# Units of the SSD stage traced behind single weight pieces, convolutions and output step among them

## The chip, the cores and the metric

The kernel runs on one core of a Trainium2 chip. The time is device microseconds of one execution, and the lower the better. The program is one launch with no communication between cores. Matmuls run on TensorE (PE in the profile), elementwise work on VectorE (DVE) and ScalarE (ACT), loads are issued by SyncE (SP).

## The reference, cut to what matters

Two decoder layers over 256 tokens of width 2048. Layer 0 is a Mamba-2 mixer (the SSD stage), layer 1 a dilated attention. The change lies in layer 0:

```python
proj = h @ in_w                                   # 2048 -> z (4096), x (4096), B and C (8 groups x 128 each), dt (64)
xBC = silu(causal_depthwise_conv(xBC, conv_w, conv_b))   # 4 taps
dt = softplus(dt + dt_bias);  A = -exp(A_log)
# one chunk of 256 tokens: for each of 8 groups g (8 heads of 64 columns each)
cb    = C[g] @ B[g].T                             # scores
decay = exp(acum[l] - acum[s]) for l >= s         # per head
y     = (cb * decay) @ (x * dt)  +  x * D         # output step
y     = y * silu(z)
y     = y * rsqrt(mean(y*y over the group) + eps) * norm_g
out   = y @ out_w                                 # 4096 -> 2048
```

## The kernel before, in words

Every product is made in three passes of half precision halves: a weight piece of 128 x 1024 numbers (512 KB) is loaded to `raw`, ACT copies it to `whi` (L100), DVE makes the remainder `wlo = raw - whi` (L102), and PE multiplies the high and low halves with those of the activations. `raw` has six buffers, `whi` and `wlo` have four each. So the copy of piece p+4 can start only when PE is through with piece p, and PE is never more than four pieces behind ACT and DVE.

The program is recorded through helpers, and a scheduler then sets the order of instructions on each engine at build time; each engine works strictly through its own list. `tc.issue_after(i)` pins instructions behind i on i's engine.

The mixer's input product is done in groups. A group's weights come in up to three products: `bc` (B and C of two groups), `xs` (x of one group) and `z` (its gate). `cm_quad` takes pieces of two k-tiles with 24 matmuls each (L151 to L153); `cm_wide`, which is used for x from group 2 on, takes pieces of four k-tiles with 8 matmuls of 512 columns and 8 of 256 (L194, L197), eight pieces for a group. Products that a first stage has begun (`begun`) have fewer pieces left.

For each group there are then these steps, and it is these that the change moves:

- the convolution `conv` of one 128-row tile: ACT scales (L389), DVE adds three taps (L392), ACT takes SiLU (L394). There are four tiles of x for a group and four of B and C for two groups;
- `scores`: two matmuls, then DVE L742 and L743;
- `stage1`: ACT makes the decays `seg` in two halves of eight RELU each (L757) and an EXP (L759), and `grow` (L761); DVE multiplies with the scores (L762). `seg` has two buffers. It ends with eight transposes of x on PE (L770), `xd` and `xo` on DVE (L772, L777) and four scalings on ACT (L781);
- `stage2`, the group's output step: 4 matmuls for `po` and 16 for `py` on PE (L791, L802), then on DVE L793, L794, L805 twice and L806 (the gate), and a square on ACT (L808);
- `stage3`: sums of squares on DVE (L813, L815), two small matmuls with ones (L818), and a reciprocal root of twelve small DVE instructions (L820, L278 to L284), sent to HBM by a POOL queue.

In the loop over g the code of one turn is written in this order: the product `bc` (on odd g), `scores`, the product `xs` of group g+1, stage3 of g-1, stage1 of g, the four convolutions of x of g+1, the product `z` of g+1, stage2 of g. Each stands between whole products. `background` puts the dot products of the adaLN gate (L320, 1 MB of weights each) between pieces. At the end the product `z` of group 7 runs with the last scores inside it, and then stage2 of group 7. The output product (`out_pieces`, L228) follows: its first pieces need `y` of group 0, 1 and so on, scaled by L871 and split by ACT L878 and DVE L879 (`ylo`). stage3 of group 7 is called there at the second piece, with high priority.

Of the kernel before, what the change touches and what calls it, by code (L numbers as in the profile page):

```python
# [9 lines left out]
F32 = mybir.dt.float32  # L10
# [13 lines left out]
G = 8  # L24
# [25 lines left out]
def trunk(ctx, tc, xT, x, c, par, cst, bias, lnrow, ada, wdt, win, wxs, wout, wk, wv, wbin, wbout, out):  # L50
# [55 lines left out]
    upcoming, ready, owed = [], [], []  # L106
# [72 lines left out]

    def cm_wide(src, dst, rate=(0, 1), moving=None, later=False, seen=lambda a: a):  # L180
# [3 lines left out]
        for q in range(KT // 4):  # L184
# [6 lines left out]
            for k in range(4):  # L191
# [4 lines left out]
                for n in range(2):  # L196
                    T.matmul(ps[n][:, 0, :], lo[:, k, n * P:n * P + P], high(kt), start=False, stop=kt == KT - 1,  # L197
                             skip_group_check=True)
            background(*rate)
        def put():  # L200
# [158 lines left out]
    with ExitStack() as cA:  # L359
# [13 lines left out]
        with ExitStack() as cS:  # L373
# [11 lines left out]
            def conv(ps, ct, dst):  # L385
# [4 lines left out]
                for j in (2, 1, 0):  # L390
                    o = 3 - j
                    V.scalar_tensor_tensor(acc[:, o:], ps[:, :L - o], w[:, j:j + 1], acc[:, o:],  # L392
                                           op0=ALU.mult, op1=ALU.add)
                S.activation(dst, acc, AF.Silu)  # L394

            def bc_conv(g, t):
                for i in range(2):
                    bc[g + i] = p0.tile([P, 2, L], F32, name="bcm", bufs=3)
                    conv(t[2 * i], 32 + g + i, bc[g + i][:, 0, :])
                    conv(t[2 * i + 1], 40 + g + i, bc[g + i][:, 1, :])  # L400

            def xs_conv(g, t):
                xs[g] = xst[g]
                for i in range(4):
                    conv(t[i], 4 * g + i, xs[g][:, i, :])
# [4 lines left out]
            def xs_wide(g):  # L410
# [6 lines left out]
                def convolve():  # L417
                    for n in range(4):
                        conv(t[:, n, :], 4 * g + n, t[:, n, :])

                return convolve

            def product(kind, g, pre=None):
# [25 lines left out]
                if kind == "xs":  # L449
                    return lambda: xs_conv(g, t)  # L450
                bc_conv(g, t)

            with ExitStack() as c0:
# [243 lines left out]
                bc_conv(0, tiles(first[0]))  # L697
                xs_conv(0, tiles(first[1]))
# [47 lines left out]
            def stage1(g, cb):  # L746

                segs, grow = [], px.tile([P, 4, P], F32, name="grow", bufs=1)
                for w in range(2):
# [15 lines left out]
                    segs.append(seg)  # L765
                xd = px.tile([P, 2, 512], F32, name="xd", bufs=1)
                for b in range(2):
                    px_ = aux.tile([P, 512], F32, name="aux")
                    for i in range(4):
                        T.transpose(px_[:, i * P:i * P + P], xs[g][:, i, b * P:b * P + P], ident)  # L770
                    heads = px_.rearrange("p (h e) -> p h e", h=HPG)
                    V.tensor_tensor(xd[:, b, :].rearrange("p (h e) -> p h e", h=HPG), heads,  # L772
                                    dtT[:, b, g * HPG:(g + 1) * HPG, None].to_broadcast([P, HPG, 64]),
                                    op=ALU.mult)
                    if b == 0:
# [714 lines left out]
```

## Time and profile before

| what | value |
|---|---|
| median of three runs | 1239.31 us (1236.56 to 1241.85) |
| the profiled execution | 1240.34 us, span 1238.5 us |
| PE busy | 1210.6 us (98% of the span) |
| DVE busy | 1026.3 us (83%) |
| ACT busy | 711.5 us (57%) |
| mean granted clock of PE | 0.994 |
| 200 to 545 us (where the change lies): PE, DVE, ACT busy | 329.5, 304.7, 269.8 of 345.0 us |

The rows of the profile give the start and length of instructions in microseconds of the span; in brackets stands the engine's idle time just ahead of them and what ended it. A window's row gives the busy time of each engine in that stretch, the count of its instructions behind x, then the clock that PE was granted (1.00 is full speed) and the DMA share. A matmul's time in a row runs on into the next one's, so pieces are measured from first matmul to first matmul.

### The profile page before, as it was taken

The page shows a single profiled execution, that of the slowest core. Times are in us where ns is not written, and L with a number is a line of the kernel's source. Part 1 is how long each engine was busy: PE and PEld are TensorE (multiplying, and loading weights), DVE is VectorE, ACT ScalarE, POOL GpSimd, SP SyncE. Part 2 cuts the span into 40 slices and gives each one's busy share as a digit, 9 for nine tenths or more (in the row PEclk, how much of TensorE's full clock was granted, in tenths as well). Part 3 has the DMA queues.
Part 4 walks back from the last instruction along what each step waited for, and adds up shares of the span by engine and source line. Part 5 has one row for each costly group of instructions (what it writes and reads, how often), then busy time and mean ns, then how long its engine had stood idle before and what let it go on. Part 6 is the DMA issues. An engine that isn't in the chain of part 4 may idle for free.

```text
span 1238.5 us, 20144 instructions
## 1 busy us (share of the span) xinstructions
PE 1210.6 (98%) x7772; PEld 1074.9 (87%) x7772; DVE 1026.3 (83%) x1450; ACT 711.5 (57%) x1056; POOL 12.5 (1%) x21
## 2 busy tenths in 40 slices
PE   8999999899999999979999999999999999999998
PEld 8999999888999998868888888888888888888886
DVE  6999987899888999999788678788996885756886
ACT  4555467787698899644344365443444844444751
POOL 0000000000000000000000000000000000000001
PEclk9999999999999999989999999999999999999999
DMA  9999976785767658689898668989997785355563
GB/s 374 421 421 422 422 273 232 250 312 162 217 227 200 153 204 209 145 255 358 324 370 337 244 221 320 352 347 361 373 392 283 276 269 175 115 188 170 189 257 68
DMA packets 81969, 337.06 MB, mean 272 GB/s; under 512 B 9537, under 2 KB 10321, under 8 KB 69073
## 3 DMA queue, kind: packets, MB, share of 16 engines
q1 hardware_dynamic: 80496, 333.59, 75.3%
q0 software_dynamic: 1168, 2.11, 1.0%
q8 instruction: 61, 1.00, 0.3%
q14 instruction: 36, 0.29, 0.1%
q10 hardware_dynamic: 208, 0.08, 0.0%
HBM read 332.50 MB, written 3.24 MB: 271 GB/s over the span
## 4 chain that ended last, share of the span: by engine, by line
PE 73%; DVE 11%; ACT 7%; DMA 6%; issue 3%; SPq 0%; DVEq 0%; ACTq 0%
PE acc L228 23%; PE acc L194 21%; PE acc L197 11%; DMA raw<-in_win 3%; DVE wlo L102 3%; DVE araw L320 3%; PE acc L153 3%; PE acc L151 3%; PE acc L152 3%; ACT whi L100 2%; DVE cacc L392 2%; DMA araw<-in_ada 2%; ACT seg L757 1%; PE py L802 1%; PE acc L238 1%
## 5 line engine op out<-in xcount | busy, mean ns | idle before, releaser
L100 ACT ACTIVATE whi<-raw 128x1024 fp32r<-128x1024 f32 x389 | 408.1, 1057 | 345.0 <-PE acc L194 105.7
L102 DVE TENSOR_TENSOR wlo<-raw,whi 128x1024 fp32r<-128x1024 f32 x389 | 470.2, 1221 | 135.9 <-ACT whi L100 130.5
L194 PE MATMUL acc<-actT,whi 128*128 128x512 f32 x1280 | 401.4, 394 | 0.0
L197 PEld LDWEIGHTS acc<-actT,wlo 128*128 128x128 f32 x1280 | 239.5, 188 | 54.5 <-DVE wlo L102 2.3
L197 PE MATMUL acc<-actT,wlo 128*128 128x256 f32 x1280 | 254.8, 280 | 1.5 <-DVE wlo L102 1.3
L153 PE MATMUL acc<-actT,wlo 128*128 128x256 f32 x884 | 242.1, 279 | 7.9 <-DVE wlo L102 7.9
L151 PE MATMUL acc<-actT,whi 128*128 128x256 f32 x884 | 245.4, 280 | 1.3 <-ACT whi L100 0.7
L152 PE MATMUL acc<-actT,whi 128*128 128x256 f32 x884 | 244.6, 278 | 0.0
L320 DVE SCALAR_TENSOR_TENSOR araw<-araw,cb__72 128x2048 f32<-128x2048 f32 x95 | 217.1, 2285 | 2.0 <-DMA araw<-in_ada 1.7
L194 PEld LDWEIGHTS acc<-actT,whi 128*128 128x128 f32 x1280 | 194.8, 188 | 0.6
L153 PEld LDWEIGHTS acc<-actT,wlo 128*128 128x128 f32 x884 | 164.8, 189 | 10.1 <-DVE wlo L102 9.9
L151 PEld LDWEIGHTS acc<-actT,whi 128*128 128x128 f32 x884 | 166.9, 189 | 2.9 <-ACT whi L100 0.9
L152 PEld LDWEIGHTS acc<-actT,whi 128*128 128x128 f32 x884 | 166.9, 189 | 0.2 <-issue 0.2
L228 PE MATMUL acc<-whi,actT 128*128 128x512 f32 x560 | 144.4, 392 | 0.5 <-ACT whi L100 0.5
L228 PEld LDWEIGHTS acc<-whi,actT 128*128 128x128 f32 x560 | 105.1, 189 | 23.0 <-ACT whi L100 0.9
L228 PE MATMUL acc<-wlo,actT 128*128 128x512 f32 x384 | 104.1, 393 | 0.0
L228 PEld LDWEIGHTS acc<-wlo,actT 128*128 128x128 f32 x384 | 72.7, 189 | 16.0
L228 PE MATMUL acc<-whi,ylo 128*128 128x512 f32 x208 | 57.4, 399 | 1.4 <-DVE ylo L879 1.4
L228 PEld LDWEIGHTS acc<-whi,ylo 128*128 128x128 f32 x208 | 39.7, 191 | 10.1 <-DVE ylo L879 1.5
L757 ACT ACTIVATE seg<-cbc,cumT 128x128 f32<-128x128 f32 x128 | 40.9, 388 | 5.1 <-PE py L802 3.4
L392 DVE SCALAR_TENSOR_TENSOR cacc<-xs,prm,cacc 128x255 f32<-128x255 f32 (+2 forms) x84 | 37.4, 478 | 2.4 <-ACT cacc L389 2.1
L524 ACT ACTIVATE htmp<-xt,mod 128x256 f32<-128x256 f32 x16 | 9.6, 600 | 31.0 <-DVE mod L325 29.3
(331 smaller groups left out, 1092.6 us busy)
## 6 DMA issues: line engine op xcount, KB each, us to landing
araw<-in_ada SPq DMA_DIRECT2D x96, 1024.0 KB, 7.5
raw<-in_win SPq DMA_DIRECT2D x109, 512.0 KB, 9.4
raw<-in_wout SPq DMA_DIRECT2D x64, 512.0 KB, 7.2
raw<-in_wbin SPq DMA_DIRECT2D x64, 512.0 KB, 4.0
raw<-in_wxs SPq DMA_DIRECT2D x48, 512.0 KB, 4.7
raw<-in_wv SPq DMA_DIRECT2D x48, 512.0 KB, 7.2
raw<-in_wk SPq DMA_DIRECT2D x48, 512.0 KB, 7.7
cbc<-cumd SPq DMA_DIRECT2D x16, 512.0 KB, 6.2
```

What stands on the lines that cost most here:

```text
L100: copied.append(S.activation(hi, raw, AF.Copy))
L102: latest.append(V.tensor_tensor(lo, raw, hi.bitcast(F32), op=ALU.subtract))
L151: T.matmul(o, hi[:, k, c_], ahi[:, kt, :], start=first, stop=False, skip_group_check=True)
L152: T.matmul(o, hi[:, k, c_], alo[:, kt, :], start=False, stop=False, skip_group_check=True)
L153: end = T.matmul(o, lo[:, k, c_], ahi[:, kt, :], start=False, stop=kt == k1 - 1, skip_group_check=True)
L194: T.matmul(ps[n], hi[:, k, n * P:n * P + P], both(kt), start=kt == 0, stop=False, skip_group_check=True)
L197: T.matmul(ps[n][:, 0, :], lo[:, k, n * P:n * P + P], high(kt), start=False, stop=kt == KT - 1, skip_group_check=True)
L228: T.matmul(ps[b], a_(kt)[:, b * P:b * P + P], w_[:, k, :], start=a_ is ahi and w_ is hi and kt == k0, stop=w_ is lo and kt == k1 - 1)
L238: end = T.matmul(o, l_, hi[:, k, :], start=False, stop=kt == k1 - 1, skip_group_check=part)
L320: return V.scalar_tensor_tensor(raw, raw, 1.0, cb_, op0=ALU.mult, op1=ALU.mult, accum_out=mod[layer][:, ct, j:j + 1])
L392: V.scalar_tensor_tensor(acc[:, o:], ps[:, :L - o], w[:, j:j + 1], acc[:, o:], op0=ALU.mult, op1=ALU.add)
L757: S.activation(seg[:, hh, b, :], cbc[:, hh, b, :], AF.Relu, bias=cumT[:, b, h0 + hh:h0 + hh + 1], scale=-1.0)
```

## The change

Steps become units in a list `chores`, and one unit is taken from it behind each weight piece of a product (from the second or third piece on), in `cm_quad` and `cm_wide`. Units are: the four convolutions of a `bc` product, the four convolutions of x, stage3 of g-1 together with `by_tokens` (the transposes with `xd` and `xo`, cut out of stage1), and stage2. What is left in the list is emptied at fixed places, and at g = 6 all of it. stage2 is now pinned on PE behind the last matmul of the newest piece in every group (before: in five of eight groups, behind the last matmul of a `cm_quad`). The DVE instructions of a unit are pinned behind the newest `wlo`. stage3 of group 7 is called at the ninth output piece and without high priority, `y_tiles` of group 7 at the seventh piece of the second chunk (before: the third).

```diff
@@ cm_quad
-            end = cm_piece(src, q, ps, ahi, alo, k0=k0, w=w)
+            z_end[:] = [cm_piece(src, q, ps, ahi, alo, k0=k0, w=w)]
             background(*rate)
-        z_end[:] = [end]
+            if chores and q > k0 // 2:
+                chores.pop(0)()
@@ cm_wide
+            z_end[:] = [end]
             background(*rate)
+            if chores and q > 0:
+                chores.pop(0)()
@@ conv
-            def conv(ps, ct, dst):
+            def conv(ps, ct, dst, after=None):
...
-                    V.scalar_tensor_tensor(acc[:, o:], ps[:, :L - o], w[:, j:j + 1], acc[:, o:],
-                                           op0=ALU.mult, op1=ALU.add)
+                    with tc.issue_after(after) if after is not None else ExitStack():
+                        V.scalar_tensor_tensor(acc[:, o:], ps[:, :L - o], w[:, j:j + 1], acc[:, o:],
+                                               op0=ALU.mult, op1=ALU.add)
@@ stage1 is cut in two
+                for i in range(4):
+                    S.activation(y[g][:, i, :], xs[g][:, i, :], AF.Copy, scale=pv("dsk")[:, 4 * g + i:4 * g + i + 1])
+                return [segs, cb, grow]
+
+            def by_tokens(g, made):
+
+                after = latest[-1].ins
                 xd = px.tile([P, 2, 512], F32, name="xd", bufs=1)
...
+                made.extend([xd, xo])
@@ stage2
-                behind = z_end[-1] if g in (0,2,3,4,7) else None
+                behind, after = z_end[-1], latest[-1].ins
@@ the loop over g
+            AT_ONCE = (G - 2,)
             for g in range(G - 1):
...
                 if g % 2 == 1:
-                    product("bc", g + 1)
+                    chores.extend(product("bc", g + 1))
                 cb = scores(g)
-                convolve = product("xs", g + 1)
-                if rs is not None:
-                    stage3(g - 1, rs)
-                st1 = stage1(g, cb)
-                convolve()
+                convs = product("xs", g + 1)
+                while chores:
+                    chores.pop(0)()
+                made = stage1(g, cb)
+
+                def unit(g=g, made=made, rs=rs):
+                    if rs is not None:
+                        stage3(g - 1, rs[0])
+                    by_tokens(g, made)
+
+                chores.append(unit)
+                chores.extend(convs)
                 if g < G - 2:
                     product("z", g + 1)
-                rs = stage2(g, *st1)
+                while unit in chores or chores and g == G - 2:
+                    chores.pop(0)()
+                rs = []
+                chores.append(lambda g=g, made=made, rs=rs: rs.append(stage2(g, *made)))
+                if g in AT_ONCE:
+                    while chores:
+                        chores.pop(0)()
@@ the output product
-            if q == 1:
-                with tc.high_priority():
-                    stage3(G - 1, rs)
+            if q == 8:
+                stage3(G - 1, rs)
```

The number of instructions stays the same but for two more table loads on ACT. Line numbers from 389 on shift (L392 becomes L397, L757 becomes L760, L772 becomes L783, L102 stays), so the rows below differ in them too.

The first place is DVE's list at the product `z` of group 1. Before:

```order
L446 TENSOR_TENSOR xs<-acc,xs 128x512 x2
L772 TENSOR_TENSOR xd<-aux,dtT 128x512
L777 TENSOR_TENSOR xo<-aux,dec 128x512
L772 TENSOR_TENSOR xd<-aux,dtT 128x512
L392 SCALAR_TENSOR_TENSOR cacc<-xs,prm,cacc 128x255 x2
L392 SCALAR_TENSOR_TENSOR cacc<-xs,prm,cacc 128x254 x2
L392 SCALAR_TENSOR_TENSOR cacc<-xs,prm,cacc 128x253 x2
L392 SCALAR_TENSOR_TENSOR cacc<-xs,prm,cacc 128x255
L102 TENSOR_TENSOR wlo<-raw,whi 128x1024
```

The same place in the changed kernel:

```order
L449 TENSOR_TENSOR xs<-acc,xs 128x512 x2
L102 TENSOR_TENSOR wlo<-raw,whi 128x1024
L397 SCALAR_TENSOR_TENSOR cacc<-xs,prm,cacc 128x255
L102 TENSOR_TENSOR wlo<-raw,whi 128x1024
L397 SCALAR_TENSOR_TENSOR cacc<-xs,prm,cacc 128x254
L397 SCALAR_TENSOR_TENSOR cacc<-xs,prm,cacc 128x255
L397 SCALAR_TENSOR_TENSOR cacc<-xs,prm,cacc 128x253
L397 SCALAR_TENSOR_TENSOR cacc<-xs,prm,cacc 128x254
L102 TENSOR_TENSOR wlo<-raw,whi 128x1024
L783 TENSOR_TENSOR xd<-aux,dtT 128x512
```

Three remainders `wlo` now stand where before `xd`, `xo` and seven taps stood ahead of one.

The second place is ACT's list within the product `z` of group 7, between the copies of its third and fourth piece. Before, between the copies of the fourth and fifth piece, stood the longest such stretch (one stage1, of group 7):

```order
L100 ACTIVATE whi<-raw 128x1024
L205 ACTIVATE xs<-acc 128x256 x2
L389 ACTIVATE cacc<-xs,prm 128x256 x2
L757 ACTIVATE seg<-cbc,cumT 128x128 x4
L394 ACTIVATE xs<-cacc 128x256 x2
L757 ACTIVATE seg<-cbc,cumT 128x128 x4
L761 ACT_TABLE_LOAD
L761 ACTIVATE grow<-cbc 64x256
L759 ACTIVATE seg<-seg 128x1024
L761 ACTIVATE grow<-cbc 64x256
L757 ACTIVATE seg<-cbc,cumT 128x128 x5
L808 ACTIVATE sz<-s_100 128x1024
```

Six rows follow there until the next `whi`. In the changed kernel the stretch begins with stage1 of group 6, as shown, and fourteen rows more follow before the next `whi`: two convolutions' ACT work, stage1 of group 7 with sixteen more L760, a second square and two further table loads:

```order
L100 ACTIVATE whi<-raw 128x1024
L764 ACT_TABLE_LOAD
L764 ACTIVATE grow<-cbc 64x256
L760 ACTIVATE seg<-cbc,cumT 128x128 x8
L209 ACTIVATE xs<-acc 128x256 x2
L818 ACTIVATE sz<-s_99 128x1024
L762 ACTIVATE seg<-seg 128x1024
L764 ACTIVATE grow<-cbc 64x256
L760 ACTIVATE seg<-cbc,cumT 128x128 x8
L764 ACTIVATE grow<-cbc 64x256
L762 ACTIVATE seg<-seg 128x1024
L764 ACTIVATE grow<-cbc 64x256
```

Two groups' stage1 and two squares now stand between two weight copies, 32 RELU where there were 16.

The third place is DVE's list behind the end of the product `z` of group 7, from the first `po` result of stage2 to the sum of squares. Before:

```order
L102 TENSOR_TENSOR wlo<-raw,whi 128x1024
L793 TENSOR_TENSOR xo<-aux,grow 128x512
L871 SCALAR_TENSOR_TENSOR s_98<-s_98,prm,s_6350 128x256
L794 TENSOR_TENSOR s_101<-xo,s_101 128x4x128
L871 SCALAR_TENSOR_TENSOR s_98<-s_98,prm,s_6350 128x256
L805 TENSOR_TENSOR s_101<-py,s_101 128x512 x2
L871 SCALAR_TENSOR_TENSOR s_98<-s_98,prm,s_6350 128x256
L806 TENSOR_TENSOR s_101<-s_101,sz 128x1024
L102 TENSOR_TENSOR wlo<-raw,whi 128x1024 x2
L813 TENSOR_TENSOR sz<-sz 128x512
L871 SCALAR_TENSOR_TENSOR s_98<-s_98,prm,s_6350 128x256
L815 TENSOR_TENSOR sz<-sz 128x256
```

In the changed kernel:

```order
L896 SCALAR_TENSOR_TENSOR s_98<-s_98,prm,s_6328 128x256 x4
L803 TENSOR_TENSOR xo<-aux,grow 128x512
L896 SCALAR_TENSOR_TENSOR s_99<-s_99,prm,s_6328 128x256
L804 TENSOR_TENSOR s_101<-xo,s_101 128x4x128
L896 SCALAR_TENSOR_TENSOR s_99<-s_99,prm,s_6328 128x256
L815 TENSOR_TENSOR s_101<-py,s_101 128x512 x2
L896 SCALAR_TENSOR_TENSOR s_99<-s_99,prm,s_6328 128x256
L816 TENSOR_TENSOR s_101<-s_101,sz 128x1024
L102 TENSOR_TENSOR wlo<-raw,whi 128x1024 x2
L823 TENSOR_TENSOR sz<-sz 128x512
L896 SCALAR_TENSOR_TENSOR s_99<-s_99,prm,s_6328 128x256
L102 TENSOR_TENSOR wlo<-raw,whi 128x1024
```

No `wlo` stands directly ahead of the `po` result any more, and one more stands ahead of the last sum (L825, the next row). On PE the small matmuls of stage3 (L818, now L828) still follow the fourth matmul of the third output piece in both kernels.

More of the change, by code (lines that the diff above doesn't have):

```diff
@@ L105, in trunk @@
     jobs, latest, copied, pin = [], [], [], [None]
-    upcoming, ready, owed = [], [], []
+    upcoming, ready, owed, chores = [], [], [], []
     def settle():
@@ L415, in xs_wide @@
                             moving=(lambda kt: hp[:, :, kt, :], hh_))
[L417 to L421, printed above, removed]
+                return [lambda n=n: conv(t[:, n, :], 4 * g + n, t[:, n, :], latest[-1].ins) for n in range(4)]
             def product(kind, g, pre=None):
@@ L786, in stage2 @@
+                made.extend([xd, xo])
+            def stage2(g, segs, cb, grow, xd, xo):
                 po = aux.tile([P, 512], F32, name="aux")
-                behind = z_end[-1] if g in (0,2,3,4,7) else None
+                behind, after = z_end[-1], latest[-1].ins
                 for i in range(4):
                     c_ = slice(i * P, i * P + P)
-                    with tc.issue_after(behind.ins) if behind is not None else ExitStack():
+                    with tc.issue_after(behind.ins):
```

49 lines of the change are left out of this document (25 added, 24 removed).

## The prediction

> **What bounds the kernel now.** I read the page first, then who PE waits for in 200 to 545 us, then windows of that stretch cut at first matmuls of pieces, then the timelines around the waits.
>
> ```profile
> span 1238.5 us, 20144 instructions
> PE 1210.6 (98%) x7772; PEld 1074.9 (87%) x7772; DVE 1026.3 (83%) x1450; ACT 711.5 (57%) x1056; POOL 12.5 (1%) x21
> ```
> ```profile
> PE aux L818 <- DVE sz L815: 5.6, 1, 5.6
> PE acc L153 <- DVE wlo L102: 4.9, 3, 3.2
> PE acc L228 <- DVE ylo L879: 1.4, 1, 1.4
> PE acc L197 <- DVE wlo L102: 1.3, 1, 1.3
> PE aux L791 <- DVE at L283: 0.9, 1, 0.9
> ```
> ```profile
> 228.55:239.06 10.51, 7.33 (x50) 7.13 (x49) 10.51 (x18) 5.34 (x8) 0.00 (x0) 0.84 0.48 144
> 270.03:274.45 4.42, 3.07 (x19) 2.37 (x17) 4.42 (x8) 4.06 (x8) 0.00 (x0) 1.00 0.85 333
> 324.73:329.02 4.29, 3.07 (x26) 2.87 (x25) 4.29 (x9) 1.67 (x3) 0.75 (x1) 1.00 0.32 109
> 375.57:386.55 10.98, 10.98 (x100) 10.98 (x98) 10.98 (x29) 6.34 (x10) 0.72 (x1) 1.00 0.52 166
> 486.57:508.74 22.17, 20.00 (x179) 18.86 (x178) 21.20 (x56) 19.62 (x39) 1.53 (x3) 1.00 0.41 94
> 526.31:542.59 16.28, 9.29 (x30) 7.22 (x29) 14.79 (x22) 7.62 (x8) 0.55 (x1) 0.69 0.74 277
> 545.33:559.07 13.74, 13.74 (x62) 11.27 (x60) 12.81 (x21) 7.36 (x8) 1.27 (x2) 1.00 0.98 189
> 352.19:374.38 22.19, 22.19 (x131) 19.52 (x130) 19.81 (x34) 22.02 (x39) 0.00 (x0) 1.00 0.64 208
> ```
>
> PE is the bound, and the change takes no matmul away; all it can move is PE's idle time. The undisturbed windows give the price of a piece: four of 24 matmuls in 10.98, 2.75 each; eight wide ones in 22.19, 2.77 each; five output pieces in 13.74, 2.75 each. Against these the five disturbed windows lose:
>
> - 228.55: two pieces in 10.51 instead of 5.49, so 5.0. The wait is 3.2 of it; the rest is the clock, granted at 0.84 on average there.
> - 270.03: one wide piece, 4.42 − 2.77 = 1.65. 324.73: 4.29 − 2.75 = 1.55.
> - 486.57: five pieces (13.7) and the small matmuls of groups 5 to 7 (about 4.7, rows below), so 18.4 of 22.17: 3.75.
> - 526.31: two output pieces (5.5) and 0.4 for L818 in 16.28, so 10.4; the clock is at 0.69.
>
> That is 22.35 us in all, the most that this change could bring here.
>
> **The change part by part.** First the wait at 228.55:
>
> ```profile
> 224.08 1.22 DVE L102 TENSOR_TENSOR wlo<-raw,whi 128x1024 fp32r<-128x1024 f32 x1 [0.30 <-ACT whi L100]
> 225.22 1.28 DVE L446 TENSOR_TENSOR xs<-acc,xs 128x512 f32<-128x512 f32 x2
> 228.21 2.84 DVE L392 SCALAR_TENSOR_TENSOR cacc<-xs,prm,cacc 128x255 f32<-128x255 f32 x7
> 230.97 1.22 DVE L102 TENSOR_TENSOR wlo<-raw,whi 128x1024 fp32r<-128x1024 f32 x1
> ```
>
> Between the starts of two remainders lie 6.9 us: the sum of x, `xd`/`xo` and seven taps. In the new order only the sum (1.2) stands there, so this remainder is ready at about 227.5, before PE asks for it at 228.8. Gain 5.0, clock included. The later pieces have one or two taps (0.4 each) in front, `xd`/`xo` two pieces on, with PE 2.75 a piece: they keep up.
>
> The loss at 270.03 is the same burst behind the first `bc` product (8.2 us between two remainders). It becomes 3.35 and 5.2 over two, which leaves a wait of about 0.9 one piece later, since 2.2 of L320 comes ahead of it. The loss at 324.73 stays nearly as it was (12 us of DVE between two remainders in z of group 3, held by the transposes on PE): 1.15. Three waits are new. In the third piece of xs of group 3, 9.3 us of DVE stands between remainders that PE meets 6.6 us apart with its lead used up: 2.3. In the second piece of z of group 4: 0.6. Behind stage2 of group 4 ACT has 17.7 us of work between three weight copies and PE 17.9 before it needs the third, whose copy and remainder take 2 more: 2.0, and 0.8 in the next piece. Together 0.9 + 1.15 + 2.3 + 0.6 + 2.8 = 7.75. These come from adding measured start-to-start times along the new lists; each holds to a microsecond or so.
>
> **The stretch before the fourth piece of z of group 7** is the large price. Rows of ACT before, and PE's small matmuls:
>
> ```profile
> 486.65 1.05 ACT L100 ACTIVATE whi<-raw 128x1024 fp32r<-128x1024 f32 x1
> 488.46 1.09 ACT L389 ACTIVATE cacc<-xs,prm 128x256 f32<-128x256 f32 x2 [0.23 <-DVE xs L206]
> 491.77 1.28 ACT L757 ACTIVATE seg<-cbc,cumT 128x128 f32<-128x128 f32 x4 [2.22 <-PE py L802]
> 494.86 1.28 ACT L761 ACT_TABLE_LOAD   x1
> 496.15 0.42 ACT L761 ACTIVATE grow<-cbc 64x256 f32<-64x256 f32 x1
> 496.48 1.04 ACT L759 ACTIVATE seg<-seg 128x1024 f32<-128x1024 f32 x1
> 503.90 3.89 ACT L100 ACTIVATE whi<-raw 128x1024 fp32r<-128x1024 f32 x4
> ```
> ```profile
> 374.38 0.50 PE L818 MATMUL py<-cc,sz 128*128 128x1 f32 x4
> 374.74 1.07 PE L770 MATMUL aux<-cc,xs 128*128 128x128 f32 x8
> 389.43 0.70 PE L739 MATMUL aux<-bcm 128*128 128x256 f32 x2
> 519.65 1.05 PE L791 MATMUL aux<-cb,xo 128*128 128x128 f32 x8
> 520.63 1.97 PE L802 MATMUL py<-seg,xd 128*64 128x128 f32 x32
> ```
>
> Start to start, a copy or EXP or square costs ACT 0.95, a RELU 0.3, `grow` 0.32, a scaling L389 0.5, a table load 1.28. Before, the longest stretch between two copies held 14 us of such work and ran 17.25 (486.65 to 503.90) for the waits in it. Now 32 RELU (9.4), four EXP, two squares and the copy itself (6.7), eight `grow` (2.6), three table loads (3.85) and the small ones (2.9) make 25.4. The copy ahead of it needs a buffer that PE frees with the seventh piece of xs of group 7. From there PE has two steps of stage2 (2.9 each, 519.65 to about 522.5), four pieces (11.0), two sets of transposes (0.8 each), scores and sums (1.3): 19.8. With the next copy (0.95) ACT is through at 26.3 at the earliest, so PE idles 6.5 at least. Walking the waits (the squares wait for DVE's L806, the second `seg` for stage2 of group 6) the next piece starts at 27.3 and gets its remainder at 28.4, 8.3 us late. So long an idle time brings the slow clock: in the rows the first episode cost 1.8 beyond its wait and the last about 2.7; I take 2.3. Sum 10.6; bounds 8.3 (6.5 + 1.8) and 14 (three more waits of 1 us, and 2.7).
>
> The Trainium skill, "ScalarE: Activation LUTs", section "What ACT_TABLE_LOAD costs", puts a switch of table at 1283 ns plus a DRAIN of about 1380 ns. By that the three loads would lengthen the stretch by another 4.1. The trace has the load at 494.86 for 1.28 and the next instruction at 496.15, with no such pause.
>
> **The last wait.** PE and DVE behind the end of z of group 7:
>
> ```profile
> 526.31 1.07 PE L228 MATMUL acc<-whi,actT 128*128 128x512 f32 x4
> 532.99 0.98 PE L818 MATMUL aux<-cc,sz 128*128 128x1 f32 x4 [5.61 <-DVE sz L815]
> 535.36 2.07 PE L228 MATMUL acc<-whi,ylo 128*128 128x512 f32 x4 [1.38 <-DVE ylo L879]
> ```
> ```profile
> 522.72 1.23 DVE L102 TENSOR_TENSOR wlo<-raw,whi 128x1024 fp32r<-128x1024 f32 x1 [2.05 <-ACT whi L100]
> 523.86 0.69 DVE L793 TENSOR_TENSOR xo<-aux,grow 128x512 f32<-128x512 f32 x1
> 532.42 0.42 DVE L815 TENSOR_TENSOR sz<-sz 128x256 f32<-128x256 f32 x1
> 534.09 1.21 DVE L879 TENSOR_TENSOR ylo<-s,actT 128x1024 fp32r<-128x1024 f32 x1
> ```
>
> stage3 is called seven pieces later, but on PE its sum stands where it stood, behind the fourth matmul of the third output piece. What changes is DVE: L793 was ready at 520.7 and began at 523.86, behind a remainder that waited for its copy. Now nothing waits ahead of it, and PE brings 1.8 more us of output matmuls behind stage2 (eight of them used to run earlier). Against that one more remainder (1.14) stands before L815. Its copy needs the buffer of the second output piece, so L815 ends about 2.7 after PE is through with that piece, and `ylo` 1.2 later; PE meanwhile has only the four matmuls, 0.9. A wait of about 2.6 stays, too short for the slow clock by the row of 324.73 (1.00). 10.4 becomes 2.6; ends: 1.5, and 10.4 if the copies are late again.
>
> DMA issues move by one to three places among the same transfers on SP; ACT's waits for weights are not where PE waits, so they cost nothing here. POOL's list is unchanged. The background dot products keep their number.
>
> **Sum.** Losses after: 7.75 + 10.6 + 2.6 = 20.95, before 22.35. The profiled execution of 1240.34 becomes 1238.9. It lies 1.0 above the median of 1239.31, so I forecast 1238.0. The change clears the old waits and builds one new one of about their size. Half a percent (6.2 us) is what a measurement of this kernel tells from no change.
>
> **The rivals.**
>
> *The small waits are hidden and the long stretch comes out at its lower bound* (faster). Then 7.75 becomes about 1 and 10.6 becomes 8.3: 9 less, 1229. For it: 375.57 to 386.55 shows PE with no loss in z of group 4, where DVE was busy all through. Against it: three of the waits need only the sums of one list, no assumption on the others. Chance 0.26, with what lies between (to 1233).
>
> *The last wait stays* (slower). If the copies behind z of group 7 are late, since ACT must load a table and then serve two gates and three splits of y in front of them, PE meets the sum 10 us early as now, the clock falls again, and 7.8 of the gain is lost: 1246. It decides once the wait passes about 3 us, since 3.2 brought the slow clock at 228.55. For it: L815 still has three remainders ahead of it. Against it: L793 starts 3 us sooner. Chance 0.24, with a long stretch nearer to 14.
>
> By the Trainium skill, "TensorE: Matmul & The Clock Gate", "Part 1: The HAM clock gate", the gate looks at windows of about 3.4 us and halves the clock after an idle one; the row at 228.55 agrees (a wait of 3.2 did it). That rule alone would leave the waits of 2.3 and 2.6 at full clock, as my sum does.
>
> *The scheduler bunches the units, so nothing is spread*: that is what the 25.4 us stretch is, and is in the sum.
>
> **How the numbers follow.** Likeliest, within half a percent: 0.50, by itself 1233 to 1243. Faster 0.26, slower 0.24. For 8 in 10 the range reaches from the first rival's 1229 to the second's 1246.
>
> **What would show it.** Right: no wait at 228 to 232; one wait of 7 to 11 us ahead of the fourth piece of z of group 7 (`acc` waiting for `whi`, then `wlo`), with PEclk below 1 behind it; ACT without a weight copy for some 26 us there; L818's successor waiting under 3 us and no slow clock behind it. Wrong: PE passes that piece with under 4 us lost, or the last wait is still above 5, or waits of over 3 us appear in groups 3 to 6 that I did not list.

## The result and the profile after

The changed kernel takes 1248.63 us (median of 6 runs, 1247.72 to 1251.51), the kernel before 1240.43 in the same comparison (6 runs, 1236.56 to 1242.50): ratio 1.0071, 95% interval 1.0052 to 1.0091. It is 8 us slower; 1238.0 had been forecast, with 1246 as the upper end. The profiled execution has these lines:

```profile
span 1247.7 us, 20140 instructions
PE 1216.0 (97%) x7772; PEld 1077.4 (86%) x7772; DVE 1027.2 (82%) x1450; ACT 716.4 (57%) x1058; POOL 12.5 (1%) x21
```

PE is busy for 5.4 us more with the same 7772 matmuls: they ran longer at half clock. Who PE waits for, 200 to 560 us (in total, times, longest):

```profile
PE acc L151 <- ACT whi L100: 4.9, 5, 2.0
PE py L828 <- DVE sz L825: 3.9, 1, 3.9
PE aux L800 <- DVE xo L788: 2.6, 1, 2.6
PE acc L153 <- DVE wlo L102: 2.5, 3, 1.2
PE aux L828 <- DVE sz L825: 1.7, 1, 1.7
```

The waits for remainders `wlo`, 4.9 and 1.3 before, come to 2.5; those for the weight copies (`whi`), 0.7 in the same stretch of the kernel before, lead with 4.9. Windows of the changed kernel at the places of the prediction (z of group 1, the old loss in x of group 2, z of group 7 up to its output step, two stretches within it, the last part):

```profile
224.99:235.47 10.48, 9.72 (x80) 9.52 (x81) 10.48 (x17) 8.00 (x12) 0.00 (x0) 1.00 0.75 245
266.87:272.39 5.52, 5.52 (x35) 4.86 (x33) 5.52 (x10) 5.45 (x10) 0.00 (x0) 1.00 0.86 298
...
487.42:532.12 44.70, 34.93 (x255) 32.96 (x253) 38.87 (x81) 34.46 (x66) 2.56 (x4) 0.81 0.44 108
493.90:500.70 6.80, 6.80 (x39) 5.90 (x38) 5.99 (x22) 6.73 (x18) 0.71 (x1) 0.50 0.40 148
511.00:521.20 10.20, 6.60 (x28) 6.25 (x29) 9.43 (x26) 7.18 (x10) 0.82 (x2) 0.50 0.31 94
535.00:550.74 15.74, 13.58 (x55) 10.70 (x54) 14.02 (x17) 9.05 (x10) 0.56 (x1) 0.89 0.73 247
```

At the first two places the clock stays at 1.00. The time went to z of group 7: 44.70 us for some 27.1 of matmuls at the undisturbed prices (eight pieces of 2.75, and 5.1 of small matmuls with the output step of group 6), so 17.6 lost, and for 17 us of it the clock was 0.50. The same stretch of the kernel before holds eight output matmuls (1.8) besides, so there 33.08 − 1.8 − 27.1 = 4.2 are lost:

```profile
486.57:519.65 33.08, 30.29 (x260) 28.56 (x258) 32.00 (x73) 22.77 (x42) 2.80 (x5) 1.00 0.50 116
```

The rows of the changed kernel there, of PE, DVE and ACT:

```profile
492.66 1.13 PE L800 MATMUL aux<-cb,xo 128*128 128x128 f32 x8 [2.60 <-DVE xo L788]
511.36 0.99 PE L828 MATMUL py<-cc,sz 128*128 128x1 f32 x4 [3.93 <-DVE sz L825]
514.40 0.58 PE L151 MATMUL acc<-actT,whi 128*128 128x256 f32 x1 [2.05 <-ACT whi L100]
516.81 0.58 PE L153 MATMUL acc<-actT,wlo 128*128 128x256 f32 x1 [1.19 <-DVE wlo L102]
```
```profile
503.79 0.42 DVE L745 TENSOR_TENSOR cb<-aux,cc 128x256 f32<-128x256 f32 x1 [2.72 <-PE aux L743]
```
```profile
484.49 1.04 ACT L100 ACTIVATE whi<-raw 128x1024 fp32r<-128x1024 f32 x1
...
507.98 1.06 ACT L818 ACTIVATE sz<-s 128x1024 f32<-128x1024 f32 x1 [1.91 <-DVE s L816]
513.30 1.99 ACT L100 ACTIVATE whi<-raw 128x1024 fp32r<-128x1024 f32 x2
```

ACT makes no weight copy from 484.49 to 513.30, 28.8 us. PE first waits 2.60 for DVE's `xo` and falls to half clock at 493.9. The slow matmuls deliver the scores late, DVE idles 2.72 for them, ACT's square idles 1.91 for DVE, the sum of group 6 comes late, PE waits 3.93 for it and falls to half clock a second time at 511.0, in front of the copy and the remainder that were late anyway. The four waits are 9.8, half of the busy time in the two slow stretches 6.7.

First matmuls of some pieces (pieces of the input product counted through; 84 begins x of group 2, 111 x of group 4, 154 z of group 7), in us:

| piece | before | after | after − before |
|---|---|---|---|
| 60 | 187.16 | 186.84 | −0.3 |
| 84 | 264.40 | 261.23 | −3.2 |
| 111 | 352.19 | 349.93 | −2.3 |
| 154 | 486.57 | 487.42 | +0.9 |
| output step of group 7 | 519.65 | 532.12 | +12.5, or +14.3 with the eight output matmuls (1.8) that the kernel before has done by then |
| fifth output piece | 542.59 | 550.74 | +8.2 |

### The profile page after: what moved, and what is told of

It is laid out like the page before. It is cut to its first block, busy times and chain, and to the rows that moved or that the text cites. A ratio compares the mean times of both kernels' runs of the same rounds, so it can differ in the third digit from the quotient of the medians.

```text
span 1247.7 us, 20140 instructions
## 1 busy us (share of the span) xinstructions
PE 1216.0 (97%) x7772; PEld 1077.4 (86%) x7772; DVE 1027.2 (82%) x1450; ACT 716.4 (57%) x1058; POOL 12.5 (1%) x21
## 4 chain that ended last, share of the span: by engine, by line
PE 53%; ACT 1%; DMA 1%; DVE 1%; issue 0%; SPq 0%; DVEq 0%; ACTq 0%
PE acc L232 23%; PE acc L195 15%; PE acc L198 8%; PE acc L242 1%; PE acc L241 1%; PE acc L240 1%; DMA sc<-in_lnrow 1%; PE acc L1096 1%; PE po L1247 1%; PE aux L1214 1%; PE po L1237 0%; PE po L1253 0%; ACT whi L100 0%; PE aux L1224 0%; PE acc L1101 0%
## 5 line engine op out<-in xcount | busy, mean ns | idle before, releaser
L102 DVE TENSOR_TENSOR wlo<-raw,whi 128x1024 fp32r<-128x1024 f32 x389 | 469.6, 1221 | 126.6 <-ACT whi L100 119.6
L232 PEld LDWEIGHTS acc<-whi,ylo 128*128 128x128 f32 x208 | 39.1, 188 | 9.0 <-DVE ylo L904 0.6
L760 ACT ACTIVATE seg<-cbc,cumT 128x128 f32<-128x128 f32 x128 | 39.8, 389 | 5.5 <-DMA cbc<-cumd 2.7
L397 DVE SCALAR_TENSOR_TENSOR cacc<-xs,prm,cacc 128x255 f32<-128x255 f32 (+2 forms) x84 | 37.7, 475 | 0.0
L765 DVE TENSOR_TENSOR seg<-seg,cb 128x1024 f32<-128x1024 f32 x16 | 19.5, 1219 | 10.1 <-ACT seg L762 10.1
```

Source lines behind the costliest of these rows:

```text
L102: latest.append(V.tensor_tensor(lo, raw, hi.bitcast(F32), op=ALU.subtract))
L232: T.matmul(ps[b], a_(kt)[:, b * P:b * P + P], w_[:, k, :], start=a_ is ahi and w_ is hi and kt == k0, stop=w_ is lo and kt == k1 - 1)
L760: S.activation(seg[:, hh, b, :], cbc[:, hh, b, :], AF.Relu, bias=cumT[:, b, h0 + hh:h0 + hh + 1], scale=-1.0)
L765: V.tensor_tensor(seg.rearrange("p h b n -> p h (b n)"), seg.rearrange("p h b n -> p h (b n)"), cb[:, 0:2, :].rearrange("p b n -> p (b n)" ...
```

## The experiments

Each is a kernel of its own, timed in five rounds beside the kernel before; "before" is the median in its comparison (1239.0, 1240.4, 1241.1, 1241.3 and 1239.9 in the five), the ratio has its 95% interval. The theories (names for the causes that the runs set against each other): A, the two groups' decays that meet on ACT between two weight copies; B, the pins; C, that the slow clock scatters the result whatever the order; D, DVE's work at the same place; E, SP's queue; F, that taking a wait away early only postpones the loss.

### Where the loss sits: e1 to e4

**e1**, changed kernel with `AT_ONCE = (G - 3, G - 2)`: all units at once for g = 5 too.

> The changed kernel with the list emptied at the end of group 5's turn too, so the output step of group 5 is recorded seven weight pieces earlier (ahead of the x product of group 7); nothing else differs. Theory A (the late output step: it holds both seg buffers, so the decays of group 6 start late and bunch with those of group 7, PE waits twice and its clock falls twice): ACT's longest stretch without a weight copy falls from 25 to about 17 us of work, the stretch behind z of group 7 costs 4 to 6 us instead of 17.6, and the time is 1235 to 1239. Rival B (the pins of every output step on PE and of the units on DVE are what costs): the time stays at 1245 or more. Rival C (the loss is at the end edits): unchanged, 1248.

Measured 1249.58, 1.0075 (1.0052 to 1.0099): no gain. In its trace z of group 7 is nearly clean (first to last piece, 154 to 161, in 24.95; in the changed kernel 41.98 with the output step of group 6, 2.9, in it). But pieces 144 to 154 take 47.2, that step included, instead of 35.9: more than half of the bunch was moved, not split. The total hides that the stretch did get shorter: pieces 144 to 161 take 72.2, in the changed kernel 77.9. The lists of the two kernels are the same up to piece 144, yet e1 comes there 6.0 late, 2.5 of it between pieces 119 and 120. Of PE's waits for copies, 200 to 565 us, the longest (2.9) is at piece 120 and the next (2.6) at 145:

```profile
PE acc L151 <- ACT whi L100: 8.2, 5, 2.9
```

**e2**, the kernel before with only stage2 of group 5 called later:

```diff
+                if g == G - 2:
+                    rs = stage2(g - 1, *st1)      # behind the product xs of group 7
...
-                rs = stage2(g, *st1)
+                if g != G - 3:
+                    rs = stage2(g, *st1)
```

> The kernel before with one step moved: the output step of group 5 is called behind the x product of group 7 instead of ahead of it; no units, no new pins. Theory A: this alone costs 7 to 14 us (1247 to 1254), with the wait ahead of the fifth or sixth piece of z of group 7 and PE's clock at half behind it. Rival B: within 3 us of the kernel before (1238 to 1243), since no pin is added.

Measured 1250.08, 1.0073 (1.0052 to 1.0095). One late output step, with no unit and no new pin, makes a loss as large as the whole change: z of group 7 takes 40.7 from its first to its last piece, before 30.4. The time lies in the range given for A, but that doesn't show A: ACT's longest stretch without a weight copy is 16.4 us there, no longer than the 17.2 of the kernel before, and PE waits for remainders and for `xo` (L770 are the transposes). Nor does it clear the pins (B): no run takes them out of the changed kernel.

```profile
PE acc L153 <- DVE wlo L102: 7.1, 4, 3.8
PE aux L770 <- DVE xo L793: 3.2, 1, 3.2
```

**e3**, the kernel before with the two calls at the end as changed (`q == 8`, `q == 6`), and **e4**, the changed kernel with them as before.

> The kernel before with the two calls at the end alone moved (sums of squares of group 7 at the ninth output piece without priority, y of group 7 at the seventh). Theory A with the order of DVE as the reason of the shorter last wait: DVE's list ahead of the last sum is as before, so the last wait stays near 8 us and the time within 2 us of before (1238 to 1242). Rival C (these calls make the last wait shorter): 5 to 7 us faster, 1233 to 1236.

> The changed kernel with those two calls put back. Theory A: the last wait stays short (3 to 6 us lost) and the time within 2 us of the changed kernel, 1247 to 1251. Rival C: the last wait returns to 10 us, 1253 to 1256.

e3 measured 1239.63, 1.0004 (0.9984 to 1.0024): the calls alone do nothing, and its sum still waits (the profiled execution, 1248.96, is the slowest of its twelve):

```profile
537.56 0.98 PE L818 MATMUL aux<-cc,sz 128*128 128x1 f32 x4 [6.01 <-DVE sz L815]
```

e4 measured 1255.67, 1.0117 (1.0094 to 1.0141), 7 above the changed kernel. Its last part takes as long as there (162 to 166 in 15.8); it is 5.5 late already at piece 154 (1.3 of it at piece 60), where the lists of the three engines are the same as in the changed kernel. So 5 us can lie between two kernels with the same order up to a place (6.0 for e1), and for such pairs only stretches can be compared, not totals. e15 shows one such place.

### The turns apart, and work left out: e5 to e8

**e5** and **e6**: each turn is written in one of the two orders by `spread[0] = g in UNITS`; the end is that of before. e5 has `UNITS = (0, 1)`, e6 `(5, 6)`.

> The changed order in the loop's first two turns only (g = 0 and 1); all later turns and the end as before. Theory A (the units help where they lie singly behind pieces, and hurt only where two groups' decays meet in z of group 7): the losses at 228 and 270 us go (5.0 and 1.65, less a wait of 0.9), all later losses stay: 1240 - 5.8 = 1234 (1232 to 1237). Rival C (the slow clock: which waits pass 3 us is settled by small shifts anywhere, so a gain early is given back later whatever the order there): 1238 to 1244.

> The opposite: the changed order in turns g = 5 and 6 only, all else as before. Theory A: the two groups' decays meet again between the same two weight copies (25.4 us of ACT work), so z of group 7 loses 17.6 instead of 3.75 and the end 4.3 instead of 10.4: 1240 + 7.7 = 1248 (1246 to 1251). Rival C: no tie to this place, 1238 to 1244.

e5 measured 1241.04, 1.0000 (0.9987 to 1.0013). It was 3.1 ahead at piece 84 and gave it back: at piece 104, the fourth of z of group 3, it is still 1.9 ahead, that piece loses 4.6 (8.9 us lie between the starts of two remainders on DVE, 320.23 and 329.17), and at 111 it is 2.1 behind. e6 measured 1243.73, 1.0022 (1.0009 to 1.0036): slower, by less than expected. Its z of group 7:

```profile
490.09:529.07 38.98, 31.46 (x255) 30.09 (x254) 36.53 (x79) 31.57 (x56) 2.55 (x4) 0.87 0.47 89
```

38.98 − 27.1 = 11.9 lost, against 4.2 before and 17.6 after. Counted from the lists, the same 25.4 us of ACT work stand between the two copies, but only one slow stretch follows (mean clock 0.87 instead of 0.81). So the order of these two turns alone costs about what the prediction had put on it (10.6). The changed kernel enters the same stretch otherwise and loses 5.7 more; which difference at the entry makes that, no run shows.

**e7**: the 32 RELU of groups 6 and 7 left out of the changed kernel. **e8**: there the four DVE products of decays and scores left out.

> The changed kernel with the 32 RELU of groups 6 and 7 left out (the EXP reads the loaded rows directly), so ACT's stretch in z of group 7 loses 9.4 us of work. Theory A (ACT's work between two weight copies sets the wait): 17.6 lost there becomes 4 to 8, so 1236 to 1241. Rival D (DVE, which has 25.6 us of its own work between two remainders there, sets it): 1246 to 1250, the waits for wlo stay and those for whi go.

> The changed kernel with the four DVE products of decays and scores of groups 6 and 7 left out (4 x 1.14 us), ACT's list unchanged (25.4 us between two copies). Theory A: 1246 to 1250, as the changed kernel. Rival D: the stretch is 3 to 4.6 us shorter and a slow-clock episode may go with it, 1241 to 1245.

e7 measured 1255.26 (1.0115, 1.0096 to 1.0134), e8 1266.56 (1.0207, 1.0188 to 1.0226): less work, more time; both expectations are missed. By stretches: both reach piece 154 late (493.08 and 491.31; after 487.42) with no work changed up to there. From 154 to the last piece of z e7 takes 37.7 (without eight output matmuls), 4.3 less than after, where A had asked for some 10; DVE's work there had hardly become less. e8 takes 42.8, no less than after, which speaks against D. e8 then loses 9 behind z, since DVE stands still for a root that came back late from HBM:

```profile
538.87 1.67 DVE L897 SCALAR_TENSOR_TENSOR s<-s,prm,s 128x256 f32<-128x256 f32 x4 [10.87 <-DMA s<-rootd]
```

So A is not the whole of it. In the changed kernel DVE is busy for 38.87 of the 44.70 us and ACT for 34.46, and each waits for the other; that this is what keeps the loss when one list is shortened is read from the rows, not shown.

### SP's queue: e9 to e12

In the changed order the two `cbc` loads of a group stand next to each other on SP, and SP waits 42.4 us in all for ACT's `grow` ahead of them (before 14.8), with weight loads behind. One edit, in four kernels: the changed one, the one before, that of e1 and that of e5. It leaves the lists of PE, DVE and ACT as they are.

```diff
-                    nc.sync.dma_start(cbc, bass.AP(
+                    nc.gpsimd.dma_start(cbc, bass.AP(
```

> The changed kernel with the sixteen cbc loads (rows for the decays) issued on POOL's queue instead of SP's; the lists of PE, DVE and ACT stay as they are. Theory E (in the changed order the two cbc loads of a group stand next to each other on SP, the second waits 4 to 8 us for ACT's grow, and the weight loads behind it are issued late; SP waits 42.4 us at cbc after, 14.8 before): ACT's waits for raw of wxs (6.1 us) and PE's losses in groups 3 to 6 go, 1239 to 1243. Theory A (ACT's decays between two weight copies in z of group 7 and in the short z products are the loss): the ACT lists are unchanged, so 1246 to 1250.

> The control: the same move of the cbc loads in the kernel before, lists of PE, DVE and ACT unchanged. Theory E: SP waits 14.8 us at cbc there and ACT never for wxs, so nothing to gain: 1238 to 1242. Theory A: the same.

> The kernel of e1 (all units popped at once for g = 4 and 5 also, so that the two groups' decays don't meet) with cbc on POOL's queue. Theory E: the loads of wxs come in time, the 7.9 us for which ACT waited for them and half of the 13 lost at 460 to 490 go: 1238 to 1243. Theory A: ACT's lists are as in e1, so 1247 to 1251.

> The kernel of e5 (the changed order in the first two turns only) with cbc on POOL's queue. Theory E: ACT waited 2.3 us for wxs in e5, so at most 2 faster than e5's 1241: 1238 to 1241. Theory F (a wait taken away early only postpones it, since DVE has hardly less to do than PE in 220 to 335 us; PE ran into the next burst with a lead of 1 to 3 us instead of 4 to 9): 1239 to 1243, with the loss at the fourth to fifth piece of z of group 3 still there.

All four became slower: 1262.51 (1.0163, 1.0140 to 1.0187), 1246.76 (1.0043, 1.0027 to 1.0059), 1256.07 (1.0119, 1.0100 to 1.0137) and 1247.25 (1.0040, 1.0024 to 1.0055). Theory E gets no support, though it isn't cleanly tested: ACT's waits for the weights of x, which the edit was to remove (6.1 us in the changed kernel), come to 13.2 in e9. In e9 PE waits for `whi` at the pieces where it did (104, 120, 145, 157), no shorter:

```profile
PE acc L151 <- ACT whi L100: 9.9, 6, 2.5
PE aux L800 <- DVE xo L788: 4.1, 1, 4.1
```

What the edit costs begins in group 0, where the first `cbc` now comes late: ACT waits 8.24 for it in e9 and 6.89 in e10.

```profile
217.03 0.40 ACT L760 ACTIVATE seg<-cbc,cumT 128x128 f32<-128x128 f32 x1 [8.24 <-DMA cbc<-cumd]
```

e10 is also a clean measurement of how a delay travels in the order of before: 7.4 behind at piece 84, 6.6 at 111 and 6.6 at 154. Late places there neither swallow nor multiply it. In e9 the delay against the changed kernel grows, 6.7 at 84, 9.0 at 111, 11.8 at 154: the new order has places where PE has no lead.

### The first place and the clock: e13 to e18

**e13**: `UNITS = (0,)`. **e14**: the kernel before with twenty matmuls into the sum's own PSUM tile (the memory that matmuls write to) ahead of the sum, overwritten by it; on PE the sum then stands ahead of the third output piece, no longer behind its fourth matmul. **e15**: eleven such matmuls, into the tile of `po`, in the changed kernel ahead of the output step of group 6. **e16**: e13 and e14 together. The edit of e14, cut:

```diff
+                for _ in range(20 if g == G - 1 else 0):
+                    with tc.issue_after(z_end[-1].ins):
+                        z_end[:] = [T.matmul(tile, h_[:, 0, 0:P], h_[:, 0:2, :], start=True, stop=True)]
```

> The changed order in turn g = 0 only, all else as before. Theory F' (in the order of before PE's lead is refilled at each output step, so a loss at one place is simply added and one taken away is simply gained; e5 lost its gain because turn 1 in the new order puts 9.5 us of DVE work ahead of one piece of z of group 3): the 5.0 at 228 us go and nothing later changes: 1235 to 1238. Rival F (a wait taken away early only postpones it, since DVE and ACT have no slack there): 1239 to 1242.

> The kernel before with twenty matmuls of 512 columns, whose result is overwritten, ahead of the last sum on PE, in its wait of 5.6 us. The wait stays; only PE is busy in it. If the slow clock behind that wait follows from PE's idle time and costs the 2.7 us worked out in the prediction: no half clock behind it, 1237 to 1239. If the clock is set by something else: the slow episode stays, 1240 to 1243.

> The changed kernel with eleven such matmuls ahead of the output step of group 6 in z of group 7, in the wait of 2.6 us that begins the first slow episode there; the scheduler then takes the rest of that step in one piece. If the slow clock makes the excess (half clock delays the scores, these DVE, these the sum, and PE waits again): the episode at 494 goes, 12 to 14 lost in the stretch instead of 17.6, 1242 to 1246. If the order alone makes it: 1247 to 1250.

> Both e13 and e14 in one kernel, a version that may beat both kernels. If places add up: the gains of e13 and e14 together, 1232 to 1236. If a gain at one place is lost at another: 1237 to 1241.

e13 measured 1240.95, 1.0004 (0.9990 to 1.0018). It is 3.9 ahead at piece 84 and 0.9 behind at piece 92:

```profile
228.00:260.50 32.50, 32.50 (x302) 32.15 (x300) 32.50 (x42) 25.28 (x44) 0.00 (x0) 1.00 0.81 262
```
```profile
271.54 0.80 PE L200 MATMUL acc<-actT,wlo 128*128 128x256 f32 x2 [4.78 <-DVE wlo L102]
```

PE and DVE are both busy for all of the 32.50 us. Without the old wait PE goes faster than DVE can follow: the remainders are ready only 0.6 to 2.2 us ahead of pieces 83 to 85 (before 3.9 to 5.5), and the same burst that cost 1.65 in x of group 2 now costs 4.78 and the slow clock (6.4 in all). Before, DVE used the wait at 228 to catch up.

e14 measured 1239.43, 0.9986 (0.9965 to 1.0007), e16 1241.52, 0.9995 (0.9978 to 1.0011): neither told from no change as a median. But in the profile of e16 the twenty matmuls cover the wait to its end, and no slow clock follows; in that of e14 the sum was ready later, 3.27 us stayed open behind the matmuls, and one followed. First the window of e16, then rows and a window of e14:

```profile
521.00:540.00 19.00, 18.65 (x117) 15.55 (x116) 17.99 (x32) 11.30 (x12) 0.56 (x1) 1.00 0.89 288
```
```profile
527.15 4.72 PE L821 MATMUL aux<-xs 128*128 128x512 f32 x20
535.14 0.58 PE L824 MATMUL aux<-cc,sz 128*128 128x1 f32 x4 [3.27 <-DVE sz L815]
...
537.00:540.40 3.40, 2.96 (x7) 2.38 (x8) 3.40 (x7) 0.85 (x1) 0.56 (x1) 0.50 0.97 360
```

The last piece of z to the fourth output piece takes 17.8 in e16, 23.0 in e14, 22.0 before. Of e14's twelve runs the five with a mean clock of 0.998 or more took 1232.5 to 1239.2, the seven below it 1236.8 to 1244.1. So the clock follows PE's idle time, which the fill seems to remove in some executions only (two were profiled).

e15 measured 1254.68, 1.0126 (1.0106 to 1.0146). In the stretch that it edits the slow clock at 494 is gone, and 154 to 161 take 39.1 instead of 42.0, with 2.5 of fill and 1.8 of output matmuls in it, so 7.2 less for the same work. But the matmuls are not what kept the clock: they stand behind the wait for `xo`, which is longer than in the changed kernel, and the clock is 1.00 all the same:

```profile
498.43 1.63 PE L799 MATMUL aux<-actT 128*128 128x512 f32 x6 [3.12 <-DVE xo L788]
...
493.40:496.81 3.41, 1.91 (x17) 1.71 (x15) 3.38 (x6) 3.41 (x10) 0.00 (x0) 1.00 0.74 246
496.81:500.23 3.42, 1.80 (x10) 1.41 (x10) 3.42 (x6) 3.37 (x10) 0.00 (x0) 1.00 0.24 90
```

And the edit changed ACT's list too: a weight copy now stands at 503.5 amid the long stretch, which becomes 13.2 and 14.5 us instead of 28.8. So the 7.2 can come from the clock or from the split, and e15 doesn't tell which. The total is worse for places ahead of the edit, where the lists are those of the changed kernel: at piece 154 it is 5.2 late, 1.6 of it lost between pieces 119 and 120 and 3.1 from piece 144 on:

```profile
461.09 0.38 PE L151 MATMUL acc<-actT,whi 128*128 128x256 f32 x1 [3.34 <-ACT whi L100]
...
462.70:466.10 3.40, 3.40 (x18) 3.40 (x17) 3.14 (x9) 2.66 (x5) 0.00 (x0) 0.50 0.70 212
```

In the changed kernel the same wait was 1.5 and no slow clock followed. Ahead of it ACT waited 0.5 and 0.4 for PE there, and in e15 1.0 and 1.8 for two weight loads. So this is one place where kernels with the same lists part: a load that is some 2 us later lengthens a wait, and the slow clock follows. Why the loads came later stays open.

**e17** and **e18**: the gate's background dot products (L320) begun in turn 2 instead of turn 1, and then put between pieces twice as often, with e13's order and with that of before.

```diff
-                if g == 1:
+                if g == 2:
                     pin[0] = latest[-1].ins
                     queue(wp1, [(0, "gate", kt) for kt in range(KT // 2)])
+                    state[0], R = 0, (1, 5)
```

> The kernel of e13 (changed order in turn 0 only) with the gate's background dot products begun in turn 2 instead of turn 1, so that five of them (11.5 us of DVE) leave 225 to 290 us for places where remainders are 5 to 10 us ahead of PE. If DVE's work is what took e13's gain back: the 3.9 stay and the loss at 270 goes too, 1234 to 1237. If a gain early is lost later whatever DVE does: 1239 to 1243.

> The control: the kernel before with the same move of the dot products. The wait at 228 comes ahead of them and stays; only the 1.65 at 270 can go: 1238 to 1240. If the dot products cost where they now stand (z of group 3, x of group 4): 1240 to 1243.

e17 measured 1241.93, 1.0018 (1.0000 to 1.0035), e18 1246.28, 1.0056 (1.0036 to 1.0076): neither is a gain. The traces answer the question all the same (that of e17, 1245.47, is the slowest of its twelve). From piece 60 to piece 92 e17 takes 96.4, e13 103.3, before 102.3, e18 102.0; from 60 to 111 e17 is 8.1 quicker than before (e18 2.5). Then both lose 8.8 in one piece (113), where the dot products now stand (in e17 one of them waited 8.39 for its load):

```profile
228.00:260.50 32.50, 32.50 (x302) 32.21 (x301) 27.09 (x38) 26.77 (x47) 0.00 (x0) 1.00 0.68 211
```
```profile
342.40 2.29 DVE L326 SCALAR_TENSOR_TENSOR araw<-araw,cb__72 128x2048 f32<-128x2048 f32 x1 [8.39 <-DMA araw<-in_ada]
```
```profile
358.65 0.80 PE L200 MATMUL acc<-actT,wlo 128*128 128x256 f32 x2 [6.53 <-DVE wlo L102]
```

With DVE at 27.1 of 32.5 instead of 32.5, the gain of turn 0 holds up to there, and only with both edits: each alone is about a microsecond or less from before at piece 92. No run gave a version that beats the kernel before; e17's order with the dot products placed elsewhere was not run.

## Why the prediction was wrong, by its steps

Its sum was −1.4; the traces differ by +8.2 at the fifth output piece. The step that failed is the long stretch in z of group 7, put at 10.6 and measured at 17.6; the first place, put at a gain of 5.0, gave 2.9.

- *The wait at 228.* Right in kind (no `wlo` wait of 3 us, clock 1.00 in both windows), wrong in size: 2.9 instead of 5.0 by piece 84. "PE 2.75 a piece: they keep up" failed: DVE is busy in 224.99 to 235.47 for 10.48 of 10.48 us, and the four pieces from 221.90 to 235.47 lose 1.8 (13.57, less 11.0 for them and 0.8 for transposes that stood ahead of them before). The deeper error is that the gain was taken as PE's own. The row for 228.55 had shown DVE at 10.51 of 10.51; e13 and e17 show that DVE's work bounds that stretch (up to piece 92, 103.3 us with it and 96.4 with 5.4 us less of it).
- *The small waits.* 84 to 111: +0.9 measured, 1.15 by the prediction's terms (1.65 of 270 gone, 0.9 and 2.3 new, 1.55 to 1.15). 111 to 154: +3.2 measured, 3.4 predicted (0.6 and 2.8). As sums right; the places are partly others: pieces 104, 120 and 145, where PE meets the end of ACT's decays, and the first piece of x of group 3 (289.14, a wait of 1.56 for DVE's `xs`), which I had not listed.
- *The long stretch in z of group 7.* This step decided it, a term of the sum that was too small: 17.6 instead of 10.6, beyond the upper bound of 14. The mechanism was right (28.8 us without a copy, 26 expected), but it is not one wait of 8.3 with 2.3 for the clock. It is four waits, 9.8, and two slow stretches, 6.7, with some 1.1 of smaller gaps. The walk let PE run at full speed up to the missing copy; in fact a shorter wait ahead of it (2.60) already halved the clock, and what PE delivers to DVE and ACT came late in turn. e6 shows the stretch at 11.9 when entered otherwise; in e15, with the first slow episode gone and a copy amid the stretch, it is 7.2 shorter. That the loop makes all of the rest is read from the rows, not shown by a run that removes nothing else, and what the pins have in it was not tested.
- *The last wait.* 1.69 and 0.47 instead of 2.6, but the slow clock came (0.89 in the last window), which I had excluded for such waits: 4.3 lost instead of 2.6. Against before (10.4) this place still gains 6.1.
- *DMA issues "cost nothing".* Whether SP's waits cost, e9 doesn't tell; but loads a little later did, through ACT, at piece 145 (e15).
- The rival that ended slower (1246) rested on the last wait, and that did go. Only its added half, a long stretch nearer to 14, pointed the right way. The median lies 2.6 beyond it.

Sum of the misses: 2.1 at the first place, 7.0 in z of group 7 (17.6 − 10.6), 1.7 at the end, less 0.4 in the small ones and 0.4 from what before lost in z of group 7 (4.2 instead of 3.75): 10.0. The measured miss is 9.6, with 0.3 gained ahead of piece 60.

## What to carry to other kernels

Before a wait is counted as gain, look at how busy the engine behind it is in that stretch: where it is full (10.51 of 10.51), the wait is its time to catch up, and removing it only moves the loss (e5, e13) until work is taken off that engine (e17, which then lost 8.8 where it put the work). A place where several lists meet may cost more than the longest list alone: here a first short wait was followed by half clock, and by the rows what PE then delivered late made the next wait. And two kernels with the same order up to a place may stand 5 us apart there, so compare stretches, not only totals: e1's total hid 5.7 us gained.

## What the runs showed of the hardware that I had not expected

- A single wait of 2.60 us was followed by half clock (0.50 from 493.9), as was one of 1.69 with 0.47 close behind it, while e15's 3.12 was not. I had read the Trainium skill, "TensorE: Matmul & The Clock Gate", "Part 1: The HAM clock gate", as asking for a whole idle window of about 3.4 us. The lengths of the slow stretches do fit windows of that size: 3.4, 6.8 and 10.2 us in all these runs, but for the one that a run's end cuts off. But the window need not be idle throughout. In the windows of 3.41 us that end where the clock fell, PE was busy for 1.24 and 1.25 (changed kernel) and 1.38 us (before, the wait at 228.55 that the prediction had read as agreeing with that rule):

```profile
490.49:493.90 3.41, 1.24 (x11) 1.27 (x12) 3.41 (x7) 3.36 (x8) 0.00 (x0) 1.00 0.10 19
541.69:545.10 3.41, 1.25 (x8) 1.09 (x8) 3.41 (x5) 1.14 (x1) 0.18 (x1) 1.00 0.84 276
...
230.21:233.62 3.41, 1.38 (x12) 1.38 (x13) 3.41 (x6) 3.27 (x5) 0.00 (x0) 1.00 0.14 22
```

e15's wait lies across two windows, with PE busy for 1.91 and 1.80. Cutting all twenty traces from 180 to 1200 us into such windows, counted from a change of the clock, gives the same: at full clock, 2.0 us of idle time or more in a window was always followed by half clock and 1.3 or less never; between the two both occur. So not the length of a wait decides, but how much of it falls into one window.
- Matmuls whose result nobody uses keep the clock up when they last to the end of the wait (e16: 1.00 throughout), and not when 3.27 us stay open behind them (e14).
- The same `cbc` load, issued on POOL's queue instead of SP's, kept ACT waiting 6.4 to 8.2 us in group 0 (1.5 to 2.8 on SP's queue in before, after and e5), and each kernel with it lost 6 to 14 us.
